# A decoder trunk's lead-in reordered: two modulation groups as TensorE rows, normalise and scale in one operation

## The chip, the cores and the metric

The kernel runs on one core of one Trainium2 chip. The metric is the device time of one execution in microseconds (us), as the median of several runs. In the profile PE is TensorE's matmuls and PEld its weight loads, DVE is VectorE, ACT is ScalarE, POOL is GpSimd, and SP is the engine that issues the DMAs.

## The reference

Two layers and a final norm over x, 1024 tokens of 1024 channels. What matters here is the start of a layer: a conditioning vector c gives a shift, a scale and a gate for every channel; the tokens are normalised, scaled and shifted, and multiplied with one wide input projection.

```python
c_act = jax.nn.silu(c)
...
mod = c_act @ w_ada + b_ada                 # (1, 3 * 1024)
shift, scale, gate = jnp.split(mod[:, None, :], 3, axis=-1)
h = rms_norm(x, norm_g) * (1.0 + scale) + shift
proj = h @ w_in
```

`rms_norm` divides each token by the root of its mean square over the 1024 channels and multiplies by `norm_g`. The rest of a layer (pooling, retention, RWKV-7 mixing, gates, output projection) follows from `proj` and is not touched by the change.

## The kernel before

**Layout.** Channels lie on the 128 partitions, tokens in the free dimension. x comes as 16 tiles of 128 channels by 512 tokens: eight K-tiles (`kt` 0 to 7, the contraction of the projection) for each of two token halves (`h` 0 and 1). Each matmul of the projection is made of three products, because both factors are split into a high part that TensorE takes at its fast fp32 rate (`hi`, type fp32r) and the rest (`lo`): hi with weight-hi, hi with weight-lo, lo with weight-hi.

**The lead-in** is the part of the program inside `manual_schedule`, lines 1277 to 1393: there each engine runs its instructions in the order in which the code writes them. It loads everything, computes the statistics and the modulation of layer 0, makes `hi` and `lo` of all 16 tiles, and multiplies them with the first three weight tiles (`mms`: 9 matmuls of 512 columns for one K-tile of one half, 144 in all). Three output tiles for two halves need six PSUM accumulators: three of the pool `acc`, one of the tile `ch`, and the two halves of the tile `two`. The same halves of `two` first hold the broadcast reciprocal roots of the two token halves. After the lead-in a planner takes over, which orders the body by costs and due times when the kernel is built.

**The steps of the lead-in**, by their helpers:
- `xdma`, `aload`, `ada_load`, `wdma` issue the loads on SP's queue, one after another. At most eight are under way: each waits for the one eight places before it. x tiles, modulation weights and weight tiles are 256 KB each.
- `sq(h, ...)`: ScalarE squares a tile, VectorE adds the squares of eight tiles (L1197, L1201). `sums(h)`: TensorE sums them over the partitions. `rstd`, `rstd_bc`, `rstd_copy`: root and reciprocal, broadcast over the partitions by TensorE into PSUM (`rbc`), and a copy in SBUF (`rbs`, L1227).
- `normed` (L1233, L1235): x times the reciprocal, on VectorE from PSUM or on POOL or VectorE from SBUF.
- `ada(0, g)`: modulation group g. Groups 0 to 3 hold the scale and shift of one K-tile each (256 columns), group 4 those of K-tiles 4 and 5, group 5 those of 6 and 7 (512 columns). `steps(gs[g], n)` advances it by n steps. Each of the first eight steps is one VectorE instruction (L233, L235) that multiplies a weight tile by one column of the condition and adds it up; the ninth sums over the partitions with TensorE (`adaps`, one matmul a column) and ends in `ada_end`: VectorE adds the bias (L252, `mod`) and makes the coefficient (1 + scale) times `norm_g` (L258, `acoef`).
- `affine` (L1241, L1242): ScalarE makes `hi`, and then x again in full precision, each as coefficient times x plus shift. `low` (L1247): `lo` = x minus `hi`.
- `wsp` (L562, L563): a weight tile's high part on ScalarE, its low part on POOL.

## Time and profile before

| | us |
|---|---|
| median of three runs | 2447.85 |
| lowest and highest run | 2443.87, 2452.75 |
| the profiled execution's own time | 2443.31 |
| its span, first to last instruction | 2441.4 |
| PE busy | 2363.0 |
| DVE, POOL, ACT busy | 1315.2, 818.5, 799.3 |

The page gives each engine's busy time with its share of the span and its count of instructions, then the span in 40 slices, each slice a digit of busy tenths. In the views by stretch a row gives the stretch, its length, then busy time and count of PE, PEld, DVE, ACT and POOL, the granted TensorE clock, the DMA share and GB/s. A row of the timeline gives start, duration, engine, line, operation, output and inputs, shapes and count, and in brackets the idle time of the engine before it with what ended it; an fp32 matmul stands there as two instructions, and the duration of a matmul includes a latency that overlaps the next one. In the view of waits a row gives who waited, for whom, the us in total, the number of waits and the longest. In the view of a tile a row gives the durations as lowest, median, highest in ns, and the first and last start in us.

### The profile page before, as it was taken

To read this page: it belongs to the slowest core of one execution; us is meant where nothing else is said; L and a number is where in the kernel's file an instruction comes from. 1 tells how busy PE (TensorE), PEld (TensorE's weight loads), DVE (VectorE), ACT (ScalarE), POOL (GpSimd) and SP (SyncE) were. 2 spreads that over 40 slices of the span, in tenths; PEclk is the share of its full clock that TensorE was granted. 3 is DMA by queue.
4 is the path that set the end of the run, shared out by engine and by line. 5 is a ranking of instruction groups with operands and counts; after the bars stand their busy time and mean duration, and the time that the engine had idled before them with its cause. 6 is when DMAs were issued, how large, how long until landed. Compare 5 with 4: busy or idle time off the path is not lost. (4 is left out here: it accounts for less than half of the span.)

```text
span 2441.4 us, 34772 instructions
## 1 busy us (share of the span) xinstructions
PE 2363.0 (97%) x13312; PEld 1912.5 (78%) x13312; DVE 1315.2 (54%) x2564; ACT 799.3 (33%) x1481; POOL 818.5 (34%) x729
## 2 busy tenths in 40 slices
PE   5989999999999999999999999999999999999998
PEld 4768778778877878777877877887787888778888
DVE  7655477367458643457455646735644674322244
ACT  5542233333234222112354324323322322212243
POOL 4321232232232323374442222323313332455241
PEclk9999999999999999999999999999999999999999
DMA  7132112111213215666531211211111122543142
GB/s 251 49 109 70 40 40 75 44 48 46 70 54 109 75 61 165 191 211 194 162 118 44 79 40 40 80 39 44 63 61 40 62 75 73 183 129 97 54 151 79
DMA packets 122487, 220.52 MB, mean 90 GB/s; under 512 B 13904, under 2 KB 17232, under 8 KB 122320
## 3 DMA queue, kind: packets, MB, share of 16 engines
q1 hardware_dynamic: 122320, 218.29, 28.1%
q8 instruction: 105, 1.72, 0.3%
q14 instruction: 62, 0.51, 0.1%
HBM read 172.89 MB, written 45.35 MB: 89 GB/s over the span
## 5 line engine op out<-in xcount | busy, mean ns | idle before, releaser
L563 POOL TENSOR_TENSOR wl<-wr,wh 128x512 fp32r<-128x512 f32 x342 | 451.1, 1319 | 1161.1 <-ACT wh L562 1091.3
L445 PE MATMUL acc<-hhi,wh 128*128 128x512 f32 x2000 | 806.3, 403 | 7.8 <-ACT gsg L1140 6.6
L445 PE MATMUL acc<-hhi,wl 128*128 128x512 f32 x2000 | 809.2, 405 | 1.5 <-POOL r L1060 1.5
L445 PE MATMUL acc<-hlo,wh 128*128 128x512 f32 x2000 | 810.4, 405 | 0.0
L445 PEld LDWEIGHTS acc<-hhi,wh 128*128 128x128 f32 x2000 | 379.9, 190 | 76.3 <-ACT gsg L1140 7.9
L445 PEld LDWEIGHTS acc<-hhi,wl 128*128 128x128 f32 x2000 | 380.0, 190 | 67.9 <-POOL r L1060 2.0
L445 PEld LDWEIGHTS acc<-hlo,wh 128*128 128x128 f32 x2000 | 380.0, 190 | 64.7 <-issue 0.7
L562 ACT CAST wh<-wr 128x512 fp32r<-128x512 f32 x342 | 211.8, 620 | 629.6 <-PE acc L445 462.4
L445 PE MATMUL acc<-olo,wh 128*128 128x512 f32 x384 | 154.6, 404 | 5.9 <-POOL olo L563 5.9
L445 PE MATMUL acc<-oG,wh 128*128 128x512 f32 x384 | 154.3, 403 | 3.2 <-ACT oG L562 1.7
L445 PE MATMUL acc<-oG,wl 128*128 128x512 f32 x384 | 152.3, 398 | 0.0
L1010 DVE TENSOR_TENSOR xst<-two,MT 64x128 f32<-64x128 f32 x128 | 37.5, 293 | 182.2 <-PE two L445 181.4
L1022 DVE SCALAR_TENSOR_TENSOR S<-ch,pc,SP 64x64 f32<-64x64 f32 x256 | 72.5, 283 | 99.0 <-PE ch L445 96.2
L1007 ACT ACTIVATE SP<-S,pc 128x128 f32<-128x128 f32 x128 | 51.4, 402 | 213.1 <-DVE S L1022 202.8
L445 PEld LDWEIGHTS acc<-olo,wh 128*128 128x128 f32 x384 | 73.3, 191 | 24.8 <-POOL olo L563 8.6
L445 PEld LDWEIGHTS acc<-oG,wh 128*128 128x128 f32 x384 | 73.1, 191 | 23.3 <-ACT oG L562 2.9
L445 PEld LDWEIGHTS acc<-oG,wl 128*128 128x128 f32 x384 | 73.6, 192 | 17.6
L1529 DVE SCALAR_TENSOR_TENSOR gs<-gs,acc 128x512 f32<-128x512 f32 x64 | 43.5, 683 | 79.2 <-PE acc L445 79.2
L939 DVE TENSOR_TENSOR tm<-MT,two 64x30 f32<-64x30 f32 (+14 forms) x240 | 76.5, 319 | 12.9 <-ACT two L932 5.6
L945 DVE TENSOR_TENSOR two<-two,tm 64x30 f32<-64x30 f32 (+14 forms) x240 | 78.9, 329 | 7.3
L1527 DVE SCALAR_TENSOR_TENSOR mrg<-gs,acc 128x512 f32<-128x512 f32 x32 | 22.0, 686 | 107.6 <-PE acc L445 107.5
L1017 DVE COPY Z<-ch 64x128 f32<-64x128 f32 x128 | 36.0, 281 | 74.4 <-PE ch L445 73.9
(287 smaller groups left out, 3688.2 us busy)
## 6 DMA issues: line engine op xcount, KB each, us to landing
wr<-in_w_all SPq DMA_DIRECT2D x364, 256.0 KB, 2.6
gd<-gsg SPq DMA_DIRECT2D x74, 256.0 KB, 2.0
gs<-gd SPq DMA_DIRECT2D x74, 256.0 KB, 3.0
wada<-in_w_ada SPq DMA_DIRECT2D x70, 256.0 KB, 3.0
ol<-od SPq DMA_DIRECT2D x64, 256.0 KB, 2.9
ringG<-in_w_ada SPq DMA_DIRECT2D x26, 256.0 KB, 5.1
x<-in_xT SPq DMA_DIRECT2D x16, 256.0 KB, 4.9
od<-po SPq DMA_DIRECT2D x16, 256.0 KB, 2.0
```

The source lines that it names most:

```text
L445: nc.tensor.matmul(out, lhsT=lhsT, rhs=rhs, start=start, stop=stop, **kw)
L562: nc.scalar.copy(hi, src)
L563: eng.tensor_tensor(lo, src, hi.bitcast(F32), op=ALU.subtract)
L939: nc.vector.tensor_tensor(pr, L3[:, i + 1 :, i : i + 1].to_broadcast([64, n, i]), M3[:, i : i + 1, 0:i].to_broadcast([64, n, i]), op=ALU.mult,
L945: nc.vector.tensor_tensor(M3[:, i + 1 :, 0:i], M3[:, i + 1 :, 0:i], pr, op=ALU.add)
L1007: nc.scalar.activation(SP, S, AF.Copy, scale=pcc)
L1010: nc.vector.tensor_tensor(xst[0:64, :], cy[64:128, 0:P], AV[:, c * P : (c + 1) * P], op=ALU.add)
L1017: nc.vector.tensor_copy(Z[0:64, c, :], ch[0:64, 0:P])
L1022: nc.vector.scalar_tensor_tensor(Sn[rw, rw], ch[rw, P + 64 * hd : P + 64 * hd + 64], pc[rw, c : c + 1], SP[rw, rw], op0=ALU.mult, op1=ALU.add,
L1527: nc.vector.scalar_tensor_tensor(m, s, 1.0, ps, op0=ALU.add, op1=ALU.mult)
L1529: nc.vector.scalar_tensor_tensor(s, s, 1.0, ps, op0=ALU.add, op1=ALU.mult)
```

## The change

Only the lead-in changes.

- Groups 0 and 2 of the modulation are summed on TensorE instead of VectorE: `pe_sum` takes one column of the condition as the stationary operand (128 rows, one column) and a weight tile's 256 columns as the moving one, eight matmuls into one PSUM row. `pe_col` copies that row to SBUF on ScalarE and turns it into columns with two matmuls against a single one, after which `ada_end` goes on as before.
- For half 0's K-tiles 0, 1, 2, 4, 5, 6, 7 and half 1's K-tiles 0, 1, 2, `scaled` multiplies x by the coefficient and by the reciprocal root in one VectorE instruction, which therefore needs the coefficient. `shifted` then adds the shift: ScalarE makes `hi`; `lo` comes from one VectorE instruction, (x + shift) - hi, for half 0, and as before from a second ScalarE pass and POOL for half 1. The other tiles keep `normed`, `affine` and `low`.
- On SP's queue group 0's four tiles, the constants and the first three weight tiles now come between half 0 and half 1 of x; group 1 and the others follow behind half 1, and the loads of the weights' second halves move up.
- The order of all steps is rewritten. The squares 1 to 7 of half 1 come after the first `shifted` of half 0; `pe_sum` of group 0 comes around `sums(0)`; group 2's row steps stand around the matmuls of K-tile 1; groups 3, 4 and 5 are advanced a few steps at a time between `scaled` and `shifted`; the last three stages run K-tile 6 of both halves before K-tile 7.

```diff
     def sums(h):
-        ssp[h] = mx("ssps")
+        ssp[h] = mx("ssps") if h else acc_ps()
...
+    def scaled(h, kt, rb):
+        x = xin[h][kt]
+        nc.vector.scalar_tensor_tensor(x, x, acoef[0][:, kt : kt + 1], rb, op0=ALU.mult, op1=ALU.mult)
+
+    def shifted(h, kt, eng=None):
+        x = xin[h][kt]
+        b = mod[0][:, SHIFT[kt] : SHIFT[kt] + 1]
+        hi, lo = hb("hhi"), hb("hlo")
+        nc.scalar.activation(hi, x, AF.Identity, bias=b)
+        h_cur[h].append((hi, lo))
+        if eng is None:
+            nc.vector.scalar_tensor_tensor(lo, x, b, hi.bitcast(F32), op0=ALU.add, op1=ALU.subtract)
+        else:
+            nc.scalar.activation(x, x, AF.Identity, bias=b)
+            low(eng, h, kt)
+
+    pes = {}
+
+    def pe_sum(g, kts, ps=None):
+        W_ = len(ADA[g][1]) * P
+        if ps is not None:
+            pes[g] = ps
+        for kt in kts:
+            i, o = divmod(kt * W_, HF)
+            mmul(pes[g][0:1, 0:W_], cact[:, kt : kt + 1], aw[g][i][:, o : o + W_], start=kt == 0, stop=kt == NKT - 1)
+
+    def pe_col(g):
+        n = len(ADA[g][1])
+        row = t_lt("ada_row")[0:1, 0 : n * P]
+        nc.scalar.copy(row, pes[g][0:1, 0 : n * P])
+        ps = mx("adaps")
+        for m in range(n):
+            mmul(ps[:, m : m + 1], row[:, m * P : (m + 1) * P], ones[0:1, :])
+        ada_end(0, g, ps)
...
         xdma(0, *range(8))
+        nc.sync.dma_start(out=vec[0], in_=vecs[0])
+        aload(0, 4)
         nc.sync.dma_start(out=cst, in_=consts[:, 0 : CST["bone"]])
-        nc.sync.dma_start(out=vec[0], in_=vecs[0])
+        wdma(0, 0, 1, 2)
         xdma(1, *range(8))
-        wdma(0, 0)
-        aload(0, 4)
-        wdma(0, 1, 2)
         aload(1, 4)
...
+        wdma(1, 0, 1, 2)
         sq(0, *range(8))
+        pe_sum(0, range(2), acc_ps())
         sums(0)
-        sq(1, 0, 1, 2)
+        pe_sum(0, range(2, 8))
+        aload(3, 2)
+        aload(4, 2)
         rstd(0)
+        derive(0)
         rstd_bc(0)
-        derive(0)
...
+        pe_col(0)
+        wsp(0, 0, 1, 2)
+        sq(1, 0)
+        scaled(0, 0, rbc[0])
         rstd_copy(0)
...
+        shifted(0, 0)
         acc6[0] = [acc_ps() for _ in range(3)]
         mms(0, 0)
+        sq(1, 1, 2, 3, 4, 5, 6, 7)
+        normed(0, 3, eng=G_)
+        sums(1)
+        rstd(1)
+        steps(gs[1], 5)
+        rstd_bc(1)
+        scaled(1, 0, rbc[1])
+        shifted(1, 0, G_)
+        rstd_copy(1)
+        steps(gs[1], 3)
...
         mms(0, 1)
+        pe_sum(2, range(4, 8))
+        pe_col(2)
+        normed(1, 3, eng=G_)
+        mms(1, 1)
+        steps(gs[3], 4)
+        for h in range(2):
+            scaled(h, 2, rbs[h])
+            shifted(h, 2, G_ if h else None)
+        steps(gs[3], 4)
...
         steps(gs[3], 1)
+        steps(gs[4], 2)
+        aload(5, 2)
+        for h in range(2):
+            affine(h, 3)
+            low(G_ if h else V, h, 3)
+        for _ in range(6):
+            steps(gs[4], 1)
+            aload(5, 1)
...
         steps(gs[4], 1)
+        steps(gs[5], 2)
+        for kt in (4, 5):
+            scaled(0, kt, rbs[0])
+            shifted(0, kt)
+            affine(1, kt)
+            low(G_, 1, kt)
+            steps(gs[5], 3)
...
         mms(0, 6)
+        mms(1, 6)
         mms(0, 7)
-        mms(1, 6)
         mms(1, 7)
```

More of the change, by code (lines that the diff above doesn't have):

```diff
@@ L1308, in trunk_kernel @@
                 ada_load(0, g, lambda _: w, aw[g], 1)
+        wdma(1, 0, 1, 2)
         sq(0, *range(8))
+        pe_sum(0, range(2), acc_ps())
         sums(0)
-        sq(1, 0, 1, 2)
+        pe_sum(0, range(2, 8))
+        aload(3, 2)
+        aload(4, 2)
         rstd(0)
+        derive(0)
         rstd_bc(0)
-        derive(0)
-        sq(1, 3, 4, 5, 6)
+        pe_col(0)
+        wsp(0, 0, 1, 2)
+        sq(1, 0)
+        scaled(0, 0, rbc[0])
         rstd_copy(0)
-        normed(0, 2, 3, eng=G_)
@@ L1318, in trunk_kernel @@
-        normed(0, 0)
-        sq(1, 7)
-        sums(1)
-        wsp(0, 0)
-        normed(0, 4, eng=G_)
-        normed(0, 1)
-        steps(gs[0], 6)
-        rstd(1)
-        steps(gs[0], 3)
-        aload(3, 2)
-        rstd_bc(1)
-        wsp(0, 1, 2)
-        steps(gs[1], 2)
-        affine(0, 0)
-        steps(gs[1], 1)
-        normed(1, 0)
-        low(V, 0, 0)
-        affine(1, 0)
-        steps(gs[1], 2)
-        normed(1, 1)
-        low(V, 1, 0)
-        steps(gs[1], 3)
-        rstd_copy(1)
+        shifted(0, 0)
@@ L1341, in trunk_kernel @@
         acc6[0] = [acc_ps() for _ in range(3)]
         mms(0, 0)
-        normed(1, 2, 3)
+        sq(1, 1, 2, 3, 4, 5, 6, 7)
[8 more added lines that the diff above has]
+        steps(gs[1], 3)
+        aload(4, 4)
         acc6[1] = [ps_c.tile([P, HF], F32, tag="ch", name=nm("acc")), cyt(), cyt()]
-        mms(1, 0, 0, 1)
+        mms(1, 0)
         steps(gs[1], 1)
-        mms(1, 0, 2)
@@ L1348, in trunk_kernel @@
-        normed(0, 5, 6, eng=G_)
-        both(1)
-        wdma(1, 0, 1, 2)
-        aload(4, 6)
-        steps(gs[2], 8)
-        mms(0, 1)
-        mms(1, 1, 0, 1)
-        steps(gs[2], 1)
-        mms(1, 1, 2)
-        wsp(1, 0)
-        normed(0, 7, eng=G_)
-        both(2)
-        steps(gs[3], 8)
+        pe_sum(2, range(4), mx("ada_ps"))
+        for h in range(2):
+            scaled(h, 1, rbs[h])
+            shifted(h, 1, G_ if h else None)
+        mms(0, 1)
+        pe_sum(2, range(4, 8))
@@ L1361, in trunk_kernel @@
+        pe_col(2)
[6 more added lines that the diff above has]
+        steps(gs[3], 4)
         aload(4, 2)
+        normed(1, 4, 5, eng=G_)
         mms(0, 2)
-        mms(1, 2, 0, 1)
+        mms(1, 2)
+        wsp(1, 0, 1, 2)
         steps(gs[3], 1)
-        mms(1, 2, 2)
-        wsp(1, 1)
-        both(3)
-        wsp(1, 2)
-        normed(1, 4, eng=G_)
@@ L1370, in trunk_kernel @@
-        astep(4, 5)
+        steps(gs[4], 2)
+        aload(5, 2)
+        for h in range(2):
+            affine(h, 3)
[3 more added lines that the diff above has]
+            aload(5, 1)
+        normed(1, 6, eng=G_)
         mms(0, 3)
-        mms(1, 3, 0, 1)
+        mms(1, 3)
         steps(gs[4], 1)
-        mms(1, 3, 2)
-        both(4)
-        normed(1, 5, eng=G_)
-        both(5)
-        astep(5)
+        steps(gs[5], 2)
[5 more added lines that the diff above has]
+            steps(gs[5], 3)
@@ L1379, in trunk_kernel @@
+        normed(1, 7, eng=G_)
         mms(0, 4)
         mms(1, 4)
-        normed(1, 6, 7, eng=V)
         mms(0, 5)
-        mms(1, 5, 0, 1)
         steps(gs[5], 1)
-        mms(1, 5, 2)
-        both(6, V)
-        both(7, V)
+        mms(1, 5)
+        for kt in (6, 7):
+            scaled(0, kt, rbs[0])
+            shifted(0, kt)
+            affine(1, kt)
+            low(G_, 1, kt)
         wprep(True)
```

## The prediction

> **What bounds the kernel now.** I read the page's engine shares and slices first, then busy time by stretch, then the waits of the lead-in, then its timeline.

> ```profile
> PE 2363.0 (97%) x13312; PEld 1912.5 (78%) x13312; DVE 1315.2 (54%) x2564; ACT 799.3 (33%) x1481; POOL 818.5 (34%) x729
> ...
> PE   5989999999999999999999999999999999999998
> ```
> ```profile
> 0.00:27.30 27.30, 8.71 (x36) 7.97 (x36) 18.17 (x39) 15.88 (x27) 11.14 (x17) 1.00 0.95 339
> 27.30:79.20 51.90, 41.63 (x173) 29.81 (x174) 36.31 (x68) 30.89 (x44) 25.20 (x25) 1.00 0.36 123
> ...
> 200.00:2425.00 2225.00, 2191.72 (x12469) 1777.99 (x12468) 1175.24 (x2312) 696.83 (x1320) 751.09 (x659) 0.99 0.27 87
> ```
> ```profile
> ACT hhi L1241 <- DVE acoef L258: 22.6, 6, 4.6
> ```

> TensorE bounds the body (2191.72 of 2225.00 us). The lead-in is another stage: up to 27.30 us TensorE works 8.71, and to 79.20 it is idle 10.3 more. Inside it ScalarE's affine waits six times, 22.6 us in all, for the coefficient that ends a modulation group. The changed kernel has the same body instruction order on every engine, so the time moves by what the end of the lead-in moves. Today's cadence, the first matmul of half 0 for K-tiles 0, 1, 2, 3, 4 and 6, and the last of the lead-in:

> ```profile
> 27.32 2.50 PE L445 MATMUL acc<-hhi,wbig 128*128 128x512 f32 x6 [0.46 <-ACT hhi L1241]
> ...
> 36.71 1.66 PE L445 MATMUL acc<-hhi,wbig 128*128 128x512 f32 x6 [0.49 <-ACT hhi L1241]
> ...
> 43.88 1.67 PE L445 MATMUL acc<-hhi,wbig 128*128 128x512 f32 x6 [1.45 <-ACT hhi L1241]
> ...
> 50.17 1.67 PE L445 MATMUL acc<-hhi,wbig 128*128 128x512 f32 x6 [0.55 <-ACT hhi L1241]
> ...
> 57.93 1.67 PE L445 MATMUL acc<-hhi,wbig 128*128 128x512 f32 x6 [0.55 <-ACT hhi L1241]
> ...
> 69.33 1.66 PE L445 MATMUL acc<-hhi,wbig 128*128 128x512 f32 x6 [0.49 <-ACT hhi L1241]
> ...
> 78.55 0.63 PE L445 MATMUL two<-hlo,wbig 128*128 128x512 f32 x2
> ```

> **The change, costed.** The prices (timeline, one DMA view, one tile view):

> ```profile
> DMA packets 1701, 3.10 MB, mean 387 GB/s; under 512 B 189, under 2 KB 189, under 8 KB 1701
> ```
> ```profile
> L1189 SPq DMA_DIRECT2D x<-in_xT x16: 327/422/432, 1.2 to 10.7; - x16
> ...
> DMA to landing us min/median/max: 2.7/4.9/5.2
> ```
> ```profile
> 6.28 4.11 ACT L1197 ACTIVATE sq<-x 128x512 f32<-128x512 f32 x6 [0.87 <-DMA x<-in_xT]
> 6.94 4.67 DVE L1201 TENSOR_TENSOR sq<-sq,sq 128x512 f32<-128x512 f32 x6 [0.80 <-ACT sq L1197]
> ...
> 11.67 1.87 PE L445 MATMUL ssps<-fixed,sq 128*128 128x1 f32 x8 [11.67 <-DVE sq L1201]
> ...
> 16.31 0.59 ACT L1227 COPY rbs<-two 128x512 f32<-128x512 f32 x1 [0.38 <-PE two L445]
> ...
> 20.18 2.59 DVE L235 SCALAR_TENSOR_TENSOR ada_ps<-ringG,cact,ada_ps 128x256 f32<-128x256 f32 x5
> ...
> 21.11 0.26 ACT L1216 ACTIVATE rn<-ssps,fixed 128x4 f32<-128x4 f32 x1 [3.18 <-PE ssps L445]
> 21.27 1.13 ACT L562 CAST wbig<-wr 128x512 fp32r<-128x512 f32 x2
> ...
> 24.81 2.06 PE L445 MATMUL two<-cst,rn 128*128 128x128 f32 x8
> ...
> 25.14 2.50 POOL L1235 TENSOR_TENSOR x<-x,rbs 128x512 f32<-128x512 f32 x2
> 25.18 1.24 DVE L258 SCALAR_TENSOR_TENSOR acoef<-mod,vec 128x1 f32<-128x1 f32 x1
> 26.45 0.81 ACT L1241 ACTIVATE hhi<-x,mod,acoef 128x512 fp32r<-128x512 f32 x1 [4.05 <-DVE acoef L258]
> ...
> 27.77 0.68 DVE L1233 TENSOR_TENSOR x<-x,two 128x512 f32<-128x512 f32 x1
> ...
> 33.86 0.74 PE L445 MATMUL two<-hhi,wbig 128*128 128x512 f32 x2 [2.87 <-DVE x L1233]
> ...
> 34.91 0.50 PE L445 MATMUL adaps<-fixed,ada_acc 128*128 128x1 f32 x4
> ...
> 49.12 0.75 DVE L233 TENSOR_SCALAR ada_ps<-ringG,cact 128x512 f32<-128x512 f32 x1
> ...
> 49.91 4.71 DVE L235 SCALAR_TENSOR_TENSOR ada_ps<-ringG,cact,ada_ps 128x512 f32<-128x512 f32 x6
> ...
> 54.66 0.75 DVE L235 SCALAR_TENSOR_TENSOR ada_acc<-ringG,cact,ada_ps 128x512 f32<-128x512 f32 x1
> ...
> 55.55 1.02 PE L445 MATMUL adaps<-fixed,ada_acc 128*128 128x1 f32 x8 [0.83 <-DVE ada_acc L235]
> ...
> 68.07 0.16 DVE L252 TENSOR_TENSOR mod<-adaps,vec 128x4 f32<-128x4 f32 x1 [2.76 <-PE adaps L445]
> ...
> 523.40 0.60 PE L451 MATMUL yt<-cst,yc 128*128 128x128 f32 x4
> ```
> ```profile
> L451 PE MATMUL yt<-cst,yc 128*128 128x128 f32 x64 | 9.6, 272 | 0.0
> ```
> ```profile
> 27.32 2.04 PE L445 MATMUL acc<-hhi,wbig 128*128 128x512 f32 x4 [0.46 <-ACT hhi L1241]
> ...
> 50.17 1.20 PE L445 MATMUL acc<-hhi,wbig 128*128 128x512 f32 x4 [0.55 <-ACT hhi L1241]
> ```

> Removed: 16 VectorE modulation steps (2.59 for five, so 0.52 each), eight normalisations there (0.68), five net low parts, and seven second passes on ScalarE (0.82). Added on VectorE: ten fused products and seven shifted low parts, at an estimated 0.70 to 0.75, between the product that reads PSUM (0.68) and the 512-column step (4.71 for six, 0.78). VectorE's total falls by about 5 us and ScalarE's by 5. But the fused product needs the coefficient, so it now lies between coefficient and affine, where nothing of VectorE lay before; a sum of busy time would miss that. I therefore follow the new order through each stage, with these prices.

> The new TensorE row (condition stationary, 256 columns moving, two passes) is not in the trace. A 128-column fp32 pass takes 0.11 late in the kernel (0.60 for four, of which the last is 0.27 by its mean) and 0.21 early (the eight at 24.81, after the first). A 256-column pass lies between that, if loading the weights sets it, and twice that. I take twice, 0.22 and 0.43, because the added length is all in the moving columns; both ends stay for the range.

> *To the first matmul.* Half 0's last tile has landed by 9.7, since its square ends at 10.39. Behind it come the vectors (0.11) and group 0 at 0.68 a tile (256 KB at 387 GB/s): the first at 10.5. TensorE takes two of the eight row steps, four slow passes, to 12.2; the sums, 1.87, to 14.1 (today they end at 13.5, so they lose 0.5); then twelve passes, 2.6 at the late rate or 5.1 at the early one. I take 3.4, the rate changing on the way: 17.5. Row copy on ScalarE 0.4 (between 0.26 and 0.59), two column matmuls 0.45, sum with bias and coefficient 0.5 with their hand-overs: 18.9. Fused product: 19.7. ScalarE, however, stands in order: row copy, three casts (1.13 for two), one square, the copy of the reciprocal, 21.0, and only then the affine, to 21.9. First matmul 21.9 against 27.32: 5.4 earlier.

> Queues moved past: SP now sends group 0 and three weight tiles ahead of half 1, whose last tile lands seven tiles later, 4.7 us: from 15.9 (issued 10.7, 5.2 to landing) to 20.6. That costs nothing while ScalarE takes the second square of half 1 only at 21.9; with that cover gone it costs up to 4.7. The loads of the weights' second column half wait for POOL's first splits (about 23), with groups 3 and 4 queued behind them on SP; those are read from 45 and 56 on, so 20 us hide it. POOL normalises six tiles instead of eight.

> *K-tile 1.* Here is the added wait: half 1's seven squares stand behind the first affine on ScalarE, their adds behind the first low part on VectorE, and group 1's steps behind both. Seven adds at 0.78 from 22.6 end at 28.1; sums at the late rate 0.9, root 0.26 and reciprocal: 29.8; five steps of group 1, 32.4; fused product, 33.1; affine, second pass and the copy of half 1's reciprocal, 35.4. That copy frees the bank that two of half 1's three sums write. Their seven remaining matmuls at 0.235 (1.67 for six less 1.20 for four, at 50.17) end at 37.1; column matmuls 0.5 (row at 34.91), coefficient 0.7, fused 0.75, affine 0.85: 39.9 against 36.71. The lead of 5.4 has turned into 3.2 late.

> *K-tile 2.* Nine matmuls 2.1, four more row steps 1.8, row copy, columns and coefficient: 45.3. Then four steps of group 3 and four small vector operations stand ahead of the fused product: 47.8; affine done at 49.4, 5.5 late.

> *K-tile 3.* Half 0's low part 0.75, half 1's fused product 0.7, its affine and second pass 1.7, POOL's low part 1.3 (half of 2.50), three matmuls 0.7: 54.6. Group 3's columns come only behind these: coefficient 55.8, affine 56.6, 6.4 late.

> *K-tile 4.* Today group 4's eight steps follow the coefficient of K-tile 3 undisturbed, 49.1 to 55.4. Now there are two steps, then a low part that waits for ScalarE's second pass (58.2), then six steps to 62.9; columns 1.02; coefficient 64.5; then two steps of group 5, fused product and affine: 67.7 against 57.93, 9.8 late.

> *K-tiles 5 and 6.* Twice low part 0.75, three steps 2.35, and fused product with affine 1.6, with group 5's columns and coefficient 1.5 before the second: 78.6 against 69.33, 9.3 late.

> *End.* 36 matmuls at 0.235 are left, 87.1; today the next tile starts at 79.0 (second matmul of the row at 78.55, plus one). 8.1 late: of today's 9.7 in this stretch 1.2 were waits for low parts, and these go.

> No collisions are in this sum. At 25.18 the coefficient took 1.24 where the like at 68.07 took 0.16, and it ended with POOL's product (25.14 plus half of 2.50). The new products and low parts also read two SBUF tensors, while POOL makes half 1's low parts: I add 1 us, of 0 to 4. Together +9.

> The sum stands against this execution's own 2443.31 (span 2441.4): 2452.3. That execution lies 4.5 under the runs' median of 2447.85, so on the median it is 2457.

> [...]

> **The rivals.**
> *A, slower still: TensorE falls back to its early rate.* Idle gaps of about 3.6 us appear before half 1's sums and before K-tile 4. For it: the first four matmuls took 2.04 against 1.20 later, so the early rate costs 0.21 a matmul, 1.9 for nine. Against it: after 2.87 of idle, at 33.86, two still took only 0.74. Two gaps, all early row steps (1.7), and one to three more collisions make +14 to +17: 2462 to 2465.
> [...] No row of before has such a gap late enough to show it.
> *B, not slower: VectorE's relief decides.* VectorE is busy 36.31 of 51.90 us in the second stretch, and group 4's steps run back to back. If it were the limit from coefficient to coefficient, 5 us less work would end the lead-in 5 earlier, 2443; with the early start kept on top, 2438. It decides from the point where VectorE never waits between two coefficients. Against it: in the new order VectorE waits for sums, columns and ScalarE at each K-tile.
> *C, it does partly what it should.* Row passes at the short price (2.1 less at the start, 0.9 at K-tile 2), and 2 of K-tile 4's delay gone: +4, 2452.

> **How the numbers follow.** The likeliest, +6 to +12 (2454 to 2460), 0.60; A 0.15, C 0.13, B 0.12. The range goes from C less half of what three runs span (2452 - 4.5) to A's end, 2447 to 2465; it leaves out B. 0.3% is 7.3 us, about what a measurement here tells from no change (the three runs span 8.9, 2443.87 to 2452.75). Slower by more: A and five sixths of the likeliest, 0.65. Faster by more: the half of B with the early start kept, 0.06. Within: 0.29.

> **What would show it.** First matmul of half 0 near 22, K-tiles 1, 4 and 6 near 40, 68 and 79, the end near 87, and from there the same length as now. Each step has its place: half 1's squares after the first affine, group 4's steps split in two and six. It is wrong if K-tile 1 starts before 36.7, if group 4's steps end before 57, or if the body changes length.

## The result, and the profile after

The changed kernel took 2459.82 us (median of six runs, 2455.98 to 2464.57) against 2449.03 for the kernel before (six runs, 2443.87 to 2453.85): a ratio of 1.0045, 95% interval 1.0027 to 1.0063. It is slower by 10.8 us, or 0.45%. The profiled execution took 2460.0, with a span of 2458.2.

The page of the changed kernel (engine shares, then TensorE's busy time and granted clock over the span in 40 slices):

```profile
PE 2378.7 (97%) x13344; PEld 1920.1 (78%) x13344; DVE 1308.5 (53%) x2552; ACT 793.1 (32%) x1476; POOL 813.7 (33%) x725
...
PE   6989999999999999999999999999999999999998
...
PEclk8999999999999999999999999999999999999999
```

VectorE has 6.7 us less to do, ScalarE 6.2 and POOL 4.8 less, and TensorE 15.7 more, for only 32 more instructions. The first slice of the clock line reads 8 and not 9, and that is the clue (that of the kernel before reads 9). Busy time of the same kernel by stretch (columns: stretch, length, busy time of PE, PEld, DVE, ACT, POOL with counts, granted clock, share and rate of the DMAs); after it, the kernel before:

```profile
18.86:22.28 3.42, 2.12 (x15) 1.48 (x12) 1.19 (x3) 2.45 (x5) 1.92 (x2) 1.00 1.05 386
22.28:42.76 20.48, 13.43 (x39) 10.19 (x40) 11.43 (x20) 7.35 (x13) 4.95 (x7) 0.50 0.66 224
42.76:66.65 23.89, 18.72 (x78) 11.73 (x76) 15.38 (x32) 9.39 (x14) 12.39 (x10) 1.00 0.24 75
66.65:70.06 3.41, 1.33 (x10) 0.97 (x8) 2.13 (x5) 0.00 (x0) 0.53 (x1) 1.00 0.87 300
70.06:76.89 6.83, 4.26 (x10) 3.40 (x11) 5.31 (x8) 2.83 (x4) 1.28 (x1) 0.50 0.24 90
76.89:92.40 15.51, 15.51 (x72) 12.52 (x71) 8.08 (x12) 9.77 (x17) 8.77 (x9) 1.00 0.07 18
```
```profile
29.19:79.02 49.83, 39.58 (x170) 28.12 (x169) 34.28 (x64) 29.19 (x43) 24.61 (x22) 1.00 0.33 112
```

From 18.86 us on, where its record of the clock begins, the changed kernel ran TensorE at half clock for 27.3 us of its lead-in; the kernel before, from 29.19 us on, at no time. The timeline of the changed kernel, TensorE's rows for group 0's row, half 1's sums and the first matmuls of half 0 for K-tiles 0, 1, 2, 3, 4 and 6, then the first of the next tile, which ends the lead-in:

```profile
10.85 1.86 PE L445 MATMUL acc<-ringG,cact 128*1 128x256 f32 x4 [10.85 <-DVE sq L1201]
...
14.44 4.92 PE L445 MATMUL acc<-ringG,cact 128*1 128x256 f32 x12
...
23.77 2.92 PE L445 MATMUL acc<-hhi,wbig 128*128 128x512 f32 x6 [2.80 <-ACT hhi L1253]
...
31.16 1.87 PE L445 MATMUL ssps<-fixed,sq 128*128 128x1 f32 x8 [3.18 <-DVE sq L1201]
...
38.70 2.07 PE L445 MATMUL two<-hhi,wbig 128*128 128x512 f32 x4
...
44.68 1.66 PE L445 MATMUL acc<-hhi,wbig 128*128 128x512 f32 x6
...
46.96 1.89 PE L445 MATMUL ada_ps<-wada,cact 128*1 128x256 f32 x8
...
53.76 1.66 PE L445 MATMUL acc<-hhi,wbig 128*128 128x512 f32 x6 [1.56 <-ACT hhi L1253]
...
61.47 1.65 PE L445 MATMUL acc<-hhi,wbig 128*128 128x512 f32 x6 [2.08 <-ACT hhi L1241]
...
72.63 2.93 PE L445 MATMUL acc<-hhi,wbig 128*128 128x512 f32 x6 [3.31 <-ACT hhi L1253]
...
83.93 1.63 PE L445 MATMUL acc<-hhi,wbig 128*128 128x512 f32 x6
...
92.40 0.40 PE L445 MATMUL acc<-hhi,wbig 128*128 128x512 f32 x1
```

The lead-in ends at 92.40, where the sum in the prediction had 87.1 and 1 for collisions, and the kernel before stood at 79.01: 13.4 us later. The early start is there (23.77 against 27.32) and is lost by K-tile 1 (44.68 against 36.71). The same six matmuls take 1.66 at full clock and 2.93 at half. The waits of the changed kernel from 23.7 to 92.4 (engine, waited-for step, us in total, times, longest) show what took the coefficient's place: the affine now waits for the fused product, eight times and longer than it waited for the coefficient before, and VectorE waits five times for TensorE's columns.

```profile
ACT hhi L1253 <- DVE x L1247: 30.1, 8, 8.0
...
DVE mod L252 <- PE adaps L445: 13.9, 5, 4.6
```

From the lead-in's end on, this execution took 2365.8 us (2458.2 - 92.40) and the profiled one of the kernel before 2362.4. A second execution of the kernel before, shown below, took 2372.4 there (2451.9 - 79.53), so these 3.4 us say nothing on the change. What follows goes by the lead-in, whose end a trace shows to a few hundredths, where a run's time does not resolve a few us.

### The profile page after: what moved, and what is told of

It is laid out like the page before. It is cut to its first block, busy times and chain, and to the rows that moved or that the text cites. A ratio compares the mean times of both kernels' runs of the same rounds, so it can differ in the third digit from the quotient of the medians.

```text
span 2458.2 us, 34811 instructions
## 1 busy us (share of the span) xinstructions
PE 2378.7 (97%) x13344; PEld 1920.1 (78%) x13344; DVE 1308.5 (53%) x2552; ACT 793.1 (32%) x1476; POOL 813.7 (33%) x725
## 5 line engine op out<-in xcount | busy, mean ns | idle before, releaser
L445 PE MATMUL acc<-hhi,wh 128*128 128x512 f32 x2000 | 807.8, 404 | 7.3 <-ACT gsg L1140 6.6
L445 PE MATMUL acc<-hhi,wl 128*128 128x512 f32 x2000 | 809.8, 405 | 1.5 <-POOL r L1060 1.5
L445 PE MATMUL acc<-hlo,wh 128*128 128x512 f32 x2000 | 811.1, 406 | 0.0
L445 PEld LDWEIGHTS acc<-hhi,wh 128*128 128x128 f32 x2000 | 380.3, 190 | 75.9 <-ACT gsg L1140 7.9
L445 PEld LDWEIGHTS acc<-hhi,wl 128*128 128x128 f32 x2000 | 380.7, 190 | 68.4 <-POOL r L1060 2.0
L445 PEld LDWEIGHTS acc<-hlo,wh 128*128 128x128 f32 x2000 | 380.6, 190 | 64.7 <-issue 0.7
L562 ACT CAST wh<-wr 128x512 fp32r<-128x512 f32 x342 | 211.8, 620 | 633.1 <-PE acc L445 435.2
L445 PE MATMUL acc<-olo,wh 128*128 128x512 f32 x384 | 154.6, 404 | 6.4 <-POOL olo L563 6.4
L445 PE MATMUL acc<-oG,wh 128*128 128x512 f32 x384 | 154.4, 403 | 4.0 <-DVE gs L1566 2.2
L445 PE MATMUL acc<-oG,wl 128*128 128x512 f32 x384 | 152.5, 399 | 0.0
L445 PEld LDWEIGHTS acc<-olo,wh 128*128 128x128 f32 x384 | 73.3, 191 | 25.3 <-POOL olo L563 9.1
L445 PEld LDWEIGHTS acc<-oG,wh 128*128 128x128 f32 x384 | 73.0, 190 | 24.6 <-ACT oG L562 2.9
L445 PEld LDWEIGHTS acc<-oG,wl 128*128 128x128 f32 x384 | 73.6, 192 | 17.6
L235 DVE SCALAR_TENSOR_TENSOR ada_acc<-wada,cact,ada_acc 128x512 f32<-128x512 f32 (+1 forms) x70 | 58.8, 841 | 32.0 <-DMA wada<-in_w_ada 31.3
```

Of the source, the lines that this page charges most:

```text
L235: nc.vector.scalar_tensor_tensor(part if kt < NKT - 1 else acc, w, cact[:, kt : kt + 1], part, op0=ALU.mult, op1=ALU.add)
L445: nc.tensor.matmul(out, lhsT=lhsT, rhs=rhs, start=start, stop=stop, **kw)
L562: nc.scalar.copy(hi, src)
```

## The experiments

All runs but one are one profiled execution each; the numbers are starts of the first matmul of half 0 per K-tile (K0, K1, ...) and the end of the lead-in. Theory 1: the lateness is a sum of pieces on one chain, TensorE's rate among them.

**Half 1's squares early.**

```diff
         rstd_bc(0)
+        sq(1, 0, 1, 2, 3)
         pe_col(0)
...
-        sq(1, 0)
         scaled(0, 0, rbc[0])
+        sq(1, 4)
         rstd_copy(0)
...
-        sq(1, 1, 2, 3, 4, 5, 6, 7)
+        sq(1, 5, 6, 7)
```

> The changed kernel, with four of half 1's squares moved ahead of the row copy on ScalarE, one ahead of the copy of the reciprocal and three left behind the first affine; nothing else moves. Measured by where the first matmul of each K-tile starts and where the lead-in ends (92.40 us in the changed kernel). Theory 1 (the lateness is a sum of pieces on one chain, and the squares behind the first affine are one of them): half 1's sums start at 28 instead of 31.16, K-tile 1 at 41 instead of 44.68, and the end comes 3 to 4 us earlier, at 88.5 to 89.5. Rival (half 1's own loads, moved behind group 0 and the weights, set its sums): the squares wait for their tiles instead, K-tile 1 stays within 1 us of 44.7, the end within 1 us of 92.4. Rival 2 (a later group's chain sets the end): K-tile 1 comes 3 earlier, but K-tile 4 and the end stay.

```profile
28.83 1.86 PE L445 MATMUL ssps<-fixed,sq 128*128 128x1 f32 x8 [0.45 <-DVE sq L1201]
42.33 1.68 PE L445 MATMUL acc<-hhi,wbig 128*128 128x512 f32 x6 [0.22 <-ACT hhi L1253]
...
89.68 0.40 PE L445 MATMUL acc<-hhi,wbig 128*128 128x512 f32 x1
```

In this run's timeline the sums came 2.3 us earlier, K1 2.35 and the end 2.7. That is somewhat less than theory 1 said. The sums waited for VectorE's last add, 0.45 us after K-tile 0's matmuls had ended; on the way two VectorE instructions, a low part and an add, ran beside POOL ones and filled 2.84 of the 3 us from 24 to 27, where such instructions take 0.75 and 0.69 without POOL beside them, and this execution's K0 lay 0.4 later (24.18). Half 1's loads, moved behind group 0 and the weights, do not set its sums. (2460.78 us, one run.)

**TensorE fed with zeros in four gaps.** `turnover` multiplies a tile of zeros into a spare accumulator.

```diff
+    def turnover(n, ps):
+        for _ in range(n):
+            mmul(ps[:, 0:P], xst, xst)
...
         sq(0, *range(8))
+        turnover(28, spare)
...
         pe_col(0)
+        turnover(10, spare)
...
         mms(0, 0)
+        turnover(14, spare)
...
+        turnover(12, mx("acc"))
         normed(1, 7, eng=G_)
```

> The changed kernel with extra 128x128 products of zeros on TensorE, whose result nobody reads: 28 from the start on, 10 behind group 0's columns, 14 behind K-tile 0 of half 0, 12 ahead of K-tile 4. They fill the idle gaps in which TensorE may have lost its rate. Theory 1 with TensorE's rate as its largest piece: the row passes take 0.22 instead of 0.43, so K-tile 0 starts at 20 to 21 instead of 23.77; half 1's sums and K-tile 0 of half 1 run at full rate as well, K-tile 1 starts at 39 to 41 instead of 44.68, and the end comes 4 to 6 us earlier, at 86.5 to 88.5. Rival (the rate depends on the time since the start or on the operands, not on the gaps): the row passes still take 0.43, the fill itself delays the sums, and the end lies between 91 and 97. Rival 2 (the rate is a side effect, the chain runs over VectorE and ScalarE): passes at 0.22, but the end within 1 us of 92.4.

K0 22.07, K1 42.23, end 89.28: 3.1 us gained, 4 to 6 expected. The stretches of this run say why:

```profile
9.88:13.29 3.41, 2.23 (x15) 1.35 (x15) 1.98 (x3) 1.05 (x2) 0.00 (x0) 1.00 1.05 392
13.29:16.70 3.41, 3.41 (x10) 1.04 (x10) 0.52 (x5) 0.26 (x1) 0.00 (x0) 0.50 1.04 383
...
30.36:40.60 10.24, 7.86 (x25) 5.77 (x25) 4.82 (x12) 2.18 (x4) 1.27 (x1) 0.50 0.53 162
```

The clock fell all the same, once right inside the row of group 0. It did so after a stretch of 3.41 us in which TensorE had still been busy for 2.23. So the fill was too thin, and the question stayed open until the denser fill below. (2456.77 us, one run.)

**Group 2 back on VectorE.**

```diff
         acc6[1] = [ps_c.tile([P, HF], F32, tag="ch", name=nm("acc")), cyt(), cyt()]
         mms(1, 0)
+        steps(gs[2], 8)
         steps(gs[1], 1)
-        pe_sum(2, range(4), mx("ada_ps"))
...
-        pe_sum(2, range(4, 8))
-        pe_col(2)
+        steps(gs[2], 1)
```

> The changed kernel with group 2 alone put back on VectorE: its eight steps behind group 1's, where VectorE was idle from 38.1 to 42.7, and its last part where TensorE's columns stood; group 0 stays a TensorE row. Theory 1: 16 row passes (1.94 and 1.89 us), the row copy and its hand-over leave the chain between K-tile 1 and K-tile 2; K-tile 1 stays at 44.7, K-tile 2 starts at 51 to 52 instead of 53.76, and the end comes 1.5 to 2.5 us earlier, 90 to 91. Rival (the row passes lie beside other work, since VectorE still has the fused products to do): K-tile 2 and the end within 0.7 us of the changed kernel's. Rival 2 (the eight steps delay group 1's coefficient): K-tile 1 later by 1 us or more.

Theory 1 missed: K2 and the end stayed. A stretch and a timeline row of this run:

```profile
22.50:49.81 27.31, 18.34 (x52) 14.23 (x53) 18.09 (x37) 9.52 (x16) 6.88 (x9) 0.50 0.49 168
```
```profile
44.84 2.93 PE L445 MATMUL acc<-hhi,wbig 128*128 128x512 f32 x6 [1.99 <-ACT hhi L1253]
```

Without the eight passes TensorE idled 2 us ahead of K-tile 1, and the half clock lasted to 49.81 instead of 42.76: the step that ended at 42.98 was busy for 3.28 of its 3.41 us and did not raise the clock, and the next one for 1.56 only. K-tile 1's matmuls then took 2.93, and what the row had cost was paid to the clock. In the changed kernel the row's passes follow group 1's columns without a gap, and the clock rises at 42.76; they cost time on the chain and save it by the clock, and the first rival's number came out for another reason than the one it gave. End 92.52. (2454.53 us, one run.)

**Half 0 without the fused product.** (K-tiles 2, 4, 5, 6 and 7 are edited like K-tile 1, with `normed` one stage ahead.)

```diff
         rstd_bc(0)
+        normed(0, 0)
         pe_col(0)
         wsp(0, 0, 1, 2)
-        sq(1, 0)
-        scaled(0, 0, rbc[0])
+        affine(0, 0)
+        low(V, 0, 0)
         rstd_copy(0)
-        shifted(0, 0)
...
-        sq(1, 1, 2, 3, 4, 5, 6, 7)
+        sq(1, 0, 1, 2, 3, 4, 5, 6, 7)
...
+        normed(0, 1)
...
-        for h in range(2):
-            scaled(h, 1, rbs[h])
-            shifted(h, 1, G_ if h else None)
+        affine(0, 1)
+        low(V, 0, 1)
+        scaled(1, 1, rbs[1])
+        shifted(1, 1, G_)
```

> The changed kernel with half 0 alone as before: its tiles are normalised ahead of the coefficient, in VectorE's idle time, and the affine takes scale and bias again, with a second pass and a plain low part. Half 1 keeps its fused products where it has them. Theory 1 (the fused product lies between coefficient and affine): the path from coefficient to first matmul is shorter by the product less 0.1 for the longer affine, 0.65 us for K-tiles 1, 2, 4 and 6 and 1.2 for K-tile 0, where the copy of the reciprocal also goes behind the affine: K-tile 1 at 43 to 44, K-tile 2 at 52 to 53, the end 2 to 3.5 us earlier, 89 to 90.5. Rival (half 0's second passes now delay half 1's affines on ScalarE by 0.8 each, and the end with them): end within 0.7 us of 92.4, or later.

K0 22.47, K1 44.36, K2 51.73, K4 69.92, end 89.16: 3.2 us gained, as theory 1 said. But this run had its half clock at other places (28.80 to 42.45, 59.52 to 66.35, 69.76 to 73.17), so that part of the gain could be the clock's. (2463.62 us, one run.)

**The clock held.** A denser fill: 32 products ahead of the row, 12 behind its columns, 22 behind K-tile 0, 2 and 7 around half 1's broadcast, 5 ahead of K-tile 2, 8 ahead of K-tile 3, 4 and 15 around group 4's columns; the order of everything else stays.

> The run with extra products of zeros showed the granted clock fall to 0.50 three times all the same, from 13.3 to 16.4, 30.4 to 40.2 and 67.9 to 71.3 us, each time some 3 us after TensorE had been idle for 0.6 to 2 us more than once. Here the fill is denser: 32 products before the row, 12 behind group 0's columns, 22 behind K-tile 0, 2 behind half 1's sums, 7 behind its reciprocal's broadcast, 5 ahead of K-tile 2, 8 ahead of K-tile 3, 4 and 15 around group 4's columns. Nothing else differs from the changed kernel. Theory 1 (the low clock is what the prediction's sum left out; the order alone costs what it was said to cost): the clock reads 1.00 from 7 us to the end of the lead-in, K-tile 0 starts at 20 to 21, K-tile 1 at 39 to 41, and the lead-in ends at 85.5 to 88 (the sum said 87.1). Rival (the order costs the 13 us by itself, with TensorE off the chain): clock 1.00, and the end at 89 or later. Rival 2 (the fill does not hold the clock): stretches at 0.50 remain.

One stretch and the timeline of this run (row passes, then K0, K1, K2, K3, K4, K6 and the end):

```profile
20.00:85.41 65.41, 59.90 (x332) 47.32 (x332) 42.20 (x73) 28.11 (x45) 26.46 (x26) 1.00 0.41 140
```
```profile
12.82 2.75 PE L445 MATMUL acc<-ringG,cact 128*1 128x256 f32 x12
...
20.00 1.67 PE L445 MATMUL acc<-hhi,wbig 128*128 128x512 f32 x6
...
38.34 1.66 PE L445 MATMUL acc<-hhi,wbig 128*128 128x512 f32 x6 [0.17 <-ACT hhi L1253]
...
47.44 1.67 PE L445 MATMUL acc<-hhi,wbig 128*128 128x512 f32 x6 [0.46 <-ACT hhi L1253]
...
55.15 1.67 PE L445 MATMUL acc<-hhi,wbig 128*128 128x512 f32 x6
...
66.63 1.64 PE L445 MATMUL acc<-hhi,wbig 128*128 128x512 f32 x6
...
76.96 1.61 PE L445 MATMUL acc<-hhi,wbig 128*128 128x512 f32 x6
...
85.40 0.40 PE L445 MATMUL acc<-hhi,wbig 128*128 128x512 f32 x1
```

Theory 1 holds: the clock read 1.00 from 5.44 us on, where its record begins, and K1 and the end came even a little ahead of its bounds. Work that computes nothing, put into idle time, gives 7.0 of the 13.4 us back; the other 6.4 (85.40 - 79.01) are the order's. These are differences of single traces, and the two pairs of unedited runs below scatter by 0.5 and 1.6. (2453.69 us, one run.)

**Group 4's steps in one piece.** (The splits' casts and low parts are issued apart here, so that POOL's low parts of K-tile 3 can go first.)

```diff
-        wsp(1, 0, 1, 2)
+        wcast(1, 0, 1, 2)
...
-        steps(gs[4], 2)
-        aload(5, 2)
         for h in range(2):
             affine(h, 3)
-            low(G_ if h else V, h, 3)
+            low(G_, h, 3)
+        wlow(1, 0, 1, 2)
-        for _ in range(6):
+        for _ in range(8):
...
-        steps(gs[5], 2)
...
-            steps(gs[5], 3)
+            steps(gs[5], 4)
```

> The changed kernel with group 4's eight steps in one piece on VectorE, with both low parts of K-tile 3 on POOL ahead of the splits of the weights' second column half (whose casts on ScalarE stay where they were), and group 5's two early steps moved behind K-tile 4's products. Theory 1 (the split of group 4's steps is a piece of the chain): the steps end at 66 to 66.5 instead of 68.1, K-tile 4 starts at 69 to 70.5 instead of 72.63, and the end comes 2 to 3 us earlier, 89.5 to 90.5. Rival (POOL's low parts arrive later and TensorE's columns of group 4 stand behind them; or the splits now come too late for K-tile 4): K-tile 4 within 1 us of 72.6, the end within 1 us of 92.4.

The timeline of this run (VectorE's last step, TensorE's columns, K4):

```profile
65.84 0.75 DVE L235 SCALAR_TENSOR_TENSOR ada_acc<-ringG,cact,ada_ps 128x512 f32<-128x512 f32 x1
...
67.62 0.95 PE L445 MATMUL adaps<-fixed,ada_acc 128*128 128x1 f32 x8
...
71.60 1.81 PE L445 MATMUL acc<-hhi,wbig 128*128 128x512 f32 x6 [3.03 <-ACT hhi L1253]
```

The steps did end 1.55 us earlier, at 66.59. Their columns, though, stand behind half 1's K-tile 3 on TensorE, which ran partly at half clock here, and began 1.0 after the steps' end. The coefficient behind them ran beside a POOL instruction and took 1.20 instead of 0.16. K4 came 1.0 earlier, and the end 0.1 (92.27); group 5's steps now start 2.6 later (72.25). The rival's numbers came out. Of its mechanism, TensorE's order is shown, while POOL's low part held TensorE up by 0.42 only; the half clock lay at other places than in the changed kernel (25.18 to 42.25, 62.73 to 66.14, 72.97 to 76.38), so the run does not tell how much is the order's. (2466.48 us, one run.)

**Group 0 back on VectorE.**

```diff
-        pe_sum(0, range(2), acc_ps())
         sums(0)
-        pe_sum(0, range(2, 8))
-        aload(3, 2)
-        aload(4, 2)
+        steps(gs[0], 3)
+        derive(0)
+        steps(gs[0], 1)
         rstd(0)
-        derive(0)
+        steps(gs[0], 4)
         rstd_bc(0)
-        pe_col(0)
+        steps(gs[0], 1)
+        aload(3, 2)
+        aload(4, 2)
```

> The changed kernel with group 0 alone put back on VectorE, its steps right behind half 0's adds, where VectorE is idle from 11.6 on; loads, fused products and group 2 stay as changed. Theory 1 (the TensorE row of group 0 at the low rate is a piece of the chain): eight steps of 0.52 end near 16, the coefficient stands at 17 to 18 instead of 21.65, K-tile 0 starts at 19 to 21 instead of 23.77; half 1's last tile lands near 20.6, so its sums can start at 27 to 28 instead of 31.16, and the end comes 2 to 4 us earlier. Rival (with less for TensorE to do, its clock stays low for longer and eats the gain, as it did when group 2 was put back on VectorE): K-tile 0 as in theory 1, but the end within 1 us of 92.4. Rival 2 (loads set the first stage): K-tile 0 within 1 us of 23.8.

K0 20.95, half 1's sums 27.61, K1 40.69, end 88.80: 3.6 us earlier. Of the change's parts, the one that was to speed up the start, the TensorE row of group 0, costs 2.8 us at the start as long as the clock is low. With the clock held the row brought K0 to 20.00; group 0 on VectorE was not run with the clock held, so which way is faster then is not shown. How much of the 3.6 is the clock's stays open, since the half clock lay elsewhere here too (from 29.28 on, after the sums). (2461.09 us, one run.)

**Half 0 without the fused product, clock held.** The edit of the earlier run of that name, with 32, 10, 22, 2, 7, 1, 8, 4 and 13 products as fill.

> With the fill the clock stayed at 1.00 and the lead-in ended at 85.41. Here half 0 goes back to normalising ahead of the coefficient (as in the run without fill, which ended at 89.16 but also had its low-clock stretches at other places), with the same kind of fill. So the two differ in the fused product alone, at one clock. Theory 1 (the fused product between coefficient and affine is a piece of the order's cost): K-tile 0 1 us or more earlier than 20.00, K-tiles 2, 4 and 6 earlier by 0.5 to 2 us, the end at 82.5 to 84. Rival (the gain of the run without fill was the clock's, whose low stretch there came 6 us later): the end at 85 to 85.8.

K0 18.88, K1 37.90, K2 45.41, K4 65.27, end 83.03: 2.4 us less than 85.40. One step at half clock remained (52.64 to 56.05), so this is a lower bound. The fused product on the path, with the copy of the reciprocal and one square that the edit moves behind the first affine, is worth at least 2.4 of the order's 6.4.

**The kernel before, fed with zeros.** 34, 3, 17, 16 and 5 products up to its first K-tile.

> The kernel before with zeros' products on TensorE up to its first K-tile: 34 ahead of half 0's sums, 3 behind them, 17 and 16 around half 1's sums, 5 behind its broadcast. In the kernel before, TensorE ran its first passes at the low rate too (the granted clock is recorded from 29.19 us on), but its sums and broadcasts lie beside VectorE's steps. Theory (VectorE sets the first stage of the kernel before, so that the low clock costs it little): K-tile 0 at 26.3 to 27.3, its first four matmuls at the full rate (0.9 less), and the lead-in's end 0.5 to 1.5 us earlier than 79.0. Rival (the clock holds the kernel before up as much as the changed one): K-tile 0 at 24.5 or earlier, the end at 76 or earlier.

```profile
30.28:33.70 3.42, 0.16 (x1) 0.00 (x0) 3.35 (x7) 0.58 (x1) 0.00 (x0) 1.00 0.91 322
33.70:40.53 6.83, 6.77 (x18) 5.18 (x19) 3.74 (x11) 3.56 (x5) 1.62 (x2) 0.50 0.17 51
```

K0 27.50 (its matmuls 1.65 for six, against 2.50), end 80.08. The start did not move, so there VectorE sets the first stage and not the clock. It did not move in sum only: half 1's sums, behind VectorE's last add, began at 20.30 instead of 19.21, and from the start of group 0's columns to K-tile 0 it took 2.44 instead of 3.36 (from 25.06 and 23.96). The size was missed on the wrong side, by these two stretches: TensorE's gap ahead of half 1's first matmuls filled one step nearly whole, and 6.83 us at half clock followed. (2457.24 us, one run.)

**Another order of the same parts.** Full fill; group 0 as a TensorE row; group 2 on VectorE; half 0 unfused; group 1's steps between half 1's adds, and K-tile 1 of half 0 ahead of half 1's K-tile 0:

```diff
-        sq(1, 1, 2, 3, 4, 5, 6, 7)
+        for kt in range(2, 8):
+            sq(1, kt)
+            steps(gs[1], 1)
...
+        affine(0, 1)
+        low(G_, 0, 1)
         scaled(1, 0, rbc[1])
         shifted(1, 0, G_)
...
+        mms(0, 1)
         mms(1, 0)
...
         mms(0, 3)
+        turnover(14, mx("acc"))
         steps(gs[4], 1)
         mms(1, 3)
```

> The changed kernel's first stage (loads, TensorE row of group 0, with fill so that the clock stays up), then another order: group 2 on VectorE; half 0 normalised ahead of the coefficient; group 1's steps between half 1's adds, so that K-tile 1 of half 0 comes before K-tile 0 of half 1; groups 2 and 3 stepped as soon as the group before is done; group 4's columns ahead of half 1's K-tile 3. Theory (what is left of the changed kernel's lateness at full clock, 85.4 against 79.0, is the place of the steps on VectorE): K-tile 0 at 19 to 20.5, K-tile 1 at 31 to 34, K-tile 2 at 40 to 43, K-tile 3 at 48 to 51, K-tile 4 at 58 to 62, and the end at 78 to 82, the time within 0.3% of the kernel before. Rival (the early start cannot be kept, since VectorE's work from K-tile 0 to K-tile 4 is what it is): the end at 83 or later.

```profile
19.56 1.96 PE L445 MATMUL acc<-hhi,wbig 128*128 128x512 f32 x6
...
33.53 1.63 PE L445 MATMUL acc<-hhi,wbig 128*128 128x512 f32 x6
...
60.61 1.64 PE L445 MATMUL acc<-hhi,wbig 128*128 128x512 f32 x6
...
78.38 0.40 PE L445 MATMUL acc<-hhi,wbig 128*128 128x512 f32 x1
```

K0, K1, K4 and the end lie in theory's bounds. The lead-in is 14.0 us shorter than the changed kernel's and 0.6 shorter than that of the kernel before, which is within the scatter of single traces. Timed in ten runs it took 2447.21 us against 2447.13 for the kernel before, a ratio of 1.000, interval 0.999 to 1.001. The early start can be kept, but in this form it is worth nothing that a run's time shows.

**Both kernels once more, unedited.**

> The kernel before once more, nothing edited. Theory: with gaps of at most 2.9 us between stretches of work it keeps the full clock from about 29 us on in most executions, and the lead-in ends within 1 us of 79.02; where a step of 3.413 us falls on the gap before half 1's first matmuls, as it did with the extra products, it can lose up to 1.5 us. Rival (the kernel before was lucky in its trace): a low stretch of 7 us or more, and an end at 81 or later.

The changed kernel's stretches, then one of the kernel before:

```profile
24.19:44.67 20.48, 14.07 (x40) 10.35 (x41) 11.85 (x21) 6.96 (x13) 4.32 (x6) 0.50 0.57 194
61.73:68.56 6.83, 5.66 (x13) 4.46 (x14) 6.32 (x9) 3.14 (x4) 6.83 (x6) 0.50 0.60 190
71.97:78.80 6.83, 4.76 (x11) 3.79 (x12) 5.18 (x8) 3.33 (x5) 1.28 (x1) 0.50 0.20 76
```
```profile
36.20:39.61 3.41, 3.25 (x9) 2.04 (x8) 3.20 (x8) 3.20 (x5) 1.30 (x1) 0.50 0.00 0
```

Ends at 94.04 (92.40 the first time) and 79.53 (79.01). The changed kernel falls to half clock each time, the second time in three stretches, the last of which ends a little past the bound given; the kernel before lost one step in this execution and none in the other. The difference between the kernels, 13.4 and 14.5, is therefore no accident of one trace, while single ends scatter by 0.5 to 1.6. (2462.38 and 2453.71 us, one run each.)

## Why the prediction was right, and where its sum was off

The time was forecast at 2457, likeliest 2454 to 2460, and came at 2459.82; slower by more than 0.3% had 0.65. That it fell into the likeliest range is in part luck: the lead-in ended 5.3 us later than the sum had it (92.40 against 87.1), and 13.4 later than in the kernel before, while the medians moved by 10.8. The stages, from the rows above:

| start of | predicted | measured | clock held |
|---|---|---|---|
| K-tile 0 | 21.9 | 23.77 | 20.00 |
| K-tile 1 | 39.9 | 44.68 | 38.34 |
| K-tile 2 | 49.4 | 53.76 | 47.44 |
| K-tile 3 | 56.6 | 61.47 | 55.15 |
| K-tile 4 | 67.7 | 72.63 | 66.63 |
| K-tile 6 | 78.6 | 83.93 | 76.96 |
| next tile | 87.1 | 92.40 | 85.40 |

- **To the first matmul.** The mechanism was right; the row's term was mis-sized. "I take 3.4, the rate changing on the way": the rate changed at 18.86, with eleven of the twelve passes begun, and the twelve took 4.92. The choice of twice a 128-column pass was right at both rates: 0.41 low (4.92 for twelve) and 0.23 full (2.75 for twelve with the clock held). The 5.4 us that the start was to gain became 3.55. From the row's end to the matmul the sum's 4.4 came out (19.36 to 23.77), but not by its path: the copy of the reciprocal waited 0.67 for the fused product, beside which the sum had let it run.
- **K-tile 1.** The added wait is the one named: squares behind the affine, adds behind the low part. The sum gave 18.0 from K-tile 0 to K-tile 1; with the clock held it is 18.3 (the adds 1.2 longer than in the sum, the rest 0.9 shorter), in the changed kernel 20.9. What failed at half clock is "sums at the late rate 0.9" and the seven matmuls "at 0.235": the sums took 1.87 and four of the matmuls 2.07, at half clock. The run with earlier squares puts the wait at 2.7, at the clocks it met.
- **K-tiles 2, 3 and 4.** Predicted steps of 9.5, 7.2 and 11.1; measured 9.1, 7.7 and 11.2; with the clock held 9.1, 7.7 and 11.5. Group 4's split was the longest of them. That mending the split alone would give the delay back, as C had it in part, did not show in the one run that tried it (0.1 at the end): the columns behind half 1's matmuls, a collision of 1.0 at the coefficient and group 5's steps are late next, and the half clock lay elsewhere.
- **K-tile 6 and the end.** Predicted 10.9 and 8.5, measured 11.3 and 8.5. The second stretch at half clock, where A put its second gap, cost little: from K-tile 4 to the end 19.8 instead of 18.8 with the clock held.
- **Collisions.** From K-tile 0 to the end the order alone took 65.4 with the clock held, and the sum without collisions 65.2. That is luck, and not a sign that there were none. Three VectorE instructions on the chain of the changed kernel ran beside POOL ones:

```profile
24.56 1.77 DVE L1201 TENSOR_TENSOR sq<-sq,sq 128x512 f32<-128x512 f32 x1
...
59.62 0.89 DVE L258 SCALAR_TENSOR_TENSOR acoef<-mod,vec 128x1 f32<-128x1 f32 x1
...
62.30 1.23 DVE L1282 TENSOR_TENSOR hlo<-x,hhi 128x512 fp32r<-128x512 f32 x1 [0.34 <-ACT x L1242]
```

  Like ones without POOL took 0.69, 0.16 and 0.69, so these three lost 2.35 us. With the clock held two VectorE instructions beside POOL ones again took 1 us or more (one fills 21 to 22, another 56 to 57). The sum's ground was that the new instructions read two SBUF tensors; no run shows that this is what matters, the runs show the times alone. The 1 us taken (of 0 to 4) was too little, and other terms of the sum were too long by about as much.
- **Rival A** was the half-right one. Its mechanism took place: the row ran at the low rate but for its last passes, and TensorE fell back twice, before K-tile 4 as named, and the other time one gap earlier than named, ahead of K-tile 0. The evidence against it, 0.74 for two matmuls after 2.87 us of idle, did not carry over: the first fall came inside a gap of 2.80. Its total (+14 to +17) is about what the two pairs of traces show in the lead-in (+13.4, +14.5), while the medians differ by 10.8. The likeliest path gave the order's part, and too little for the clock.
- **Rival B** is refuted: VectorE has 6.7 us less to do and the lead-in ends 13.4 later. Less work did not help an engine that waits between two coefficients; the waits view shows VectorE waiting 13.9 us for TensorE's columns, and the affine 30.1 us for the fused product behind them.

The stretches at half clock in these runs are, among others, 20.48, 6.83, 10.24 and 3.41 us long: six, two, three and one times 3.413 (20.48 / 6). TensorE was not idle throughout ahead of a fall: in the changed kernel it was busy for 2.12 of 3.42 us ahead of the first, and for 1.33 of 3.41 ahead of the second.

## What to carry to other kernels

In a stage full of short waits, ask of each new TensorE step not only how long it takes but also how busy it leaves the engine behind it: in the changed kernel the clock fell to 0.50 after 3.42 us with 2.12 of work and after 3.41 with 1.33. A sum of durations taken at full clock leaves the clock's part out, here 7.0 of 13.4 us. Work moved to an idle engine costs what that engine's present rate makes it: the row's twelve passes took 4.92 us in the changed kernel and 2.75 with the clock held. And taking work away can cost as much where the clock then stays low, as in the run with group 2 back on VectorE (half clock up to 49.81 instead of 42.76, the end at 92.52 instead of 92.40). To tell the clock's part from the order's, fill the gaps with work that nobody reads and look at the same rows again.

## What had not been expected

- **When the clock fell.** It fell after steps with 2.12, 1.33 and 2.23 us of TensorE work, and in the second execution of the kernel before after 1.82; in the first it did not after 1.80:

```profile
29.19:32.60 3.41, 1.80 (x8) 1.13 (x6) 3.30 (x8) 1.51 (x3) 0.04 (x1) 1.00 1.03 375
```

  So busy time alone does not say it. That step held 512-column products alone; the ones that lost the clock held, among others, products with one column on one side (row passes, sums, columns). Over the lead-ins of these runs, where the clock is on record, steps with 512-column products alone kept the clock from 1.65 us up (59.82 to 63.23 in the changed kernel) and lost it with 1.44 and less (57.14 to 60.56 in the run with earlier squares), while steps with others among them lost it with up to 2.28 (66.35 to 69.76 in the first run without half 0's fused product). Whether the one-column products are the reason was not tried, and stays open. Busy time was not enough in the body of the kernel before: there the clock fell after a step that was busy throughout, most of it with products of 32 by 32 (two groups of 64, which began at 229.38 and 232.18 and took 2.21 and 2.40):

```profile
230.57:233.98 3.41, 3.41 (x92) 3.00 (x89) 0.00 (x0) 1.72 (x3) 0.00 (x0) 1.00 0.02 5
233.98:237.40 3.42, 3.42 (x20) 2.77 (x18) 0.00 (x0) 1.70 (x4) 1.28 (x1) 0.50 0.01 4
```
- **It rose after full or nearly full steps.** At 42.76 and 76.89 in the changed kernel, and after 13.29 to 16.70 in the first run with zeros, where nearly all of the step was row passes: 3.41 of 3.41 busy. In the second execution of the kernel before 3.25 was enough, and 2.99 in the run with group 4's steps in one piece, while 3.28 was not with group 2 back on VectorE. So here too busy time alone does not say it.
- **What the clock column leaves out.** It reads 1.00 up to the first change that the trace recorded. In the changed kernel the passes from 10.85 on ran at 0.41 to 0.47 each under a column that reads 1.00; the kernel before likewise took 1.87 for sums that take 1.05 when fed. The durations tell the clock there, not the column.
- **The two executions of the kernel before differ in clock.** The mean granted clock was 0.989 and 0.984 in the two executions of the kernel before, 2441.4 and 2451.9 us long. If the clock was always at one of the two levels that the stretches above show, 1.00 and 0.50, that is an estimated 54 and 78 us at half rate (twice one minus the clock, times the span), or 12 us of lost time between them where 10.5 were seen. Their lead-ins differ by 0.5.
